# A hybrid encoder block: the norm's scale behind the input product, and the MLP's joints in another program order

## The chip, the cores and the metric

The kernel runs on one core of one Trainium2 chip. Its engines are TensorE (PE, with its weight loads as PEld), VectorE (DVE), ScalarE (ACT), GpSimd (POOL) and SyncE (SP), which here only issues transfers. The metric is the device time of one execution in microseconds.

## The reference, cut to what matters

One layer over x of 1024 rows and 1024 columns, float32. Two branches read the same product z, an attention with latent projections and a two-sided gated delta rule; their gated sum goes through `w_out` and is added to x, and a squared-ReLU MLP with its own norm follows.

```python
h = _rmsnorm(x, norm1_w[l])
z = h @ w_in[l]                      # 1024 x 4528, split into c_q, c_kv, k_r, gdn_qkv, gates ...
q_nope, q_rope = q[..., :MLA_NOPE], _rope(q[..., MLA_NOPE:], positions)
o_a = _mla_attention(q_nope, q_rope, k_nope, k_rope, v_a)
qkv = jax.nn.silu(conv(gdn_qkv))     # 5 taps along the rows
sol = lax.linalg.triangular_solve(a_mat, rhs, ...)   # inside the chunked delta rule
x = x + merged @ w_out[l]
h2 = _rmsnorm(x, norm2_w[l])
x = x + jnp.square(jax.nn.relu(h2 @ w_ff1[l])) @ w_ff2[l]
return _rmsnorm(x, final_norm_w)
```

## The kernel before

Everything is kept transposed: features on the 128 partitions, the 1024 rows of x along the free axis, so a tile is 128 x 1024. A float32 product is made from rounded parts: `split` (L169) casts an operand to its rounded half on ScalarE and takes the rest on VectorE, `wtile` (L144) does the same to a weight tile, and `mm3` (L159) sums three passes, high by high, high by low, low by high: 48 matmuls of 512 columns for a tile of z. A matmul on float32 operands that are not rounded is run as two instructions.

The 36 tiles of z come from `z_tile`. The first two are multiplied from the unrounded x while x is still arriving, and their results are scaled with `r1`, the inverse root mean square of each row (L247). For the others x is first scaled (L251) and split. What each tile is used for is a step (`s_k`, `s_v`, `s_q` convolve; `s_g` is a gate; `lora_norm` the latent parts; `s_m` the small rest); `ORDER` is the list of steps, one letter each. The v and q tiles and the latent parts are first copied out of PSUM by ScalarE (L270), the gates are activated straight from PSUM (L533); the k tiles are convolved out of PSUM (tiles 0 and 1 from their scaled copy). `s_s` and `s_i` are the triangular solve on VectorE (L519, L521); its result goes through DRAM (`d_x`) and comes back in `s_z`, whose first product is L661. `s_r` makes the rotary tables on 64 partitions of 1024 columns (L431 is its inner step) and stores them through ScalarE's queue. Pools with a fixed count of tiles (`mem` 35, `fill` 5, six half tiles) decide when a transfer may begin, and each engine works off a list that is fixed ahead.

The MLP multiplies half-size blocks with seven products instead of eight (`Visit`, with `order` naming them); `run` prepares the weights three products ahead (L1107, L1108). Sixteen visits make the hidden activations, `ff1_done` combines, squares and stores them to `d_u`. Products go in order 1, 5, 2, 3, 6, 7, 4 in the first visit. Then `plain` loads the activations of blocks 12 and 13 and eight whole products of 24 matmuls use them (L1415); fifteen visits of growing and shrinking depth follow, whose activations `u_prep` loads (L1322) and splits (L1323, L1324); the last two blocks are multiplied in four `PIECES` of 256 rows, each followed by the final norm (`finish`, L1451 to L1458).

## Time and profile before

| | |
|---|---|
| median of 3 runs | 1679.72 us (1675.71 to 1683.51) |
| the profiled execution | 1680.28 us, span 1678.6 us |
| TensorE busy | 1609.9 us |
| VectorE, ScalarE, GpSimd busy | 1206.8, 806.4, 222.8 us |
| mean granted clock of TensorE | 0.984 |

Times in rows are microseconds from the start of the span. A matmul's end is modelled, so neighbouring matmuls overlap in the rows, and the distance of their starts is what one costs. `L157` is a line of the kernel, often that of a helper; names such as `ps_z` are tiles, with their numbers left out. "[4.25 <-ACT u L1248]" is idle time of the engine before the row, and what ended it. SPq, ACTq and POOL rows of kind DMA are issues of transfers.

### The profile page before, as it was taken

Reading aid. Unit: us, or ns where it says so; the run is one execution under the profiler, and the core shown is the slowest. Engines: PE = TensorE matmul, PEld = TensorE weight load, DVE = VectorE, ACT = ScalarE, POOL = GpSimd, SP = SyncE. Lnnn points to the kernel's source line nnn. Section 1 sums busy time; section 2 is a strip of 40 time slices with the busy share of each in tenths; the row PEclk is TensorE's granted clock in tenths of the full one; section 3 lists DMA queues with packets and bytes.
Section 4 is the critical chain, followed back from the end, with each engine's and each line's share of the span. In section 5 each row is a group of like instructions: output and inputs, shape, how many; then the busy total and the mean of one; then the engine's idle time right before and its main releaser. Section 6 shows DMA issues by size and latency. Waiting matters only on the chain.

```text
span 1678.6 us, 21771 instructions
## 1 busy us (share of the span) xinstructions
PE 1609.9 (96%) x8201; PEld 1329.0 (79%) x8201; DVE 1206.8 (72%) x1751; ACT 806.4 (48%) x1365; POOL 222.8 (13%) x247
## 2 busy tenths in 40 slices
PE   8899999999989889999999998999999998999997
PEld 3687788877768877888878886888888777888886
DVE  5987999931335668888887668767776478788766
ACT  5567431441335558878762345444444443444333
POOL 1212100000003446545300000000000000000012
PEclk9999999999989999999999999999999999999998
DMA  4135243472234252111074211444343543444213
GB/s 180 62 108 132 80 163 113 139 213 88 76 101 132 57 163 89 39 39 39 26 250 138 89 50 56 164 149 152 138 165 118 190 167 113 163 163 145 82 57 101
DMA packets 85657, 196.87 MB, mean 117 GB/s; under 512 B 20128, under 2 KB 35744, under 8 KB 85296
## 3 DMA queue, kind: packets, MB, share of 16 engines
q1 hardware_dynamic: 61376, 153.95, 27.4%
q10 hardware_dynamic: 23360, 38.02, 6.5%
q0 software_dynamic: 816, 3.51, 1.0%
q8 instruction: 65, 1.06, 0.3%
q14 instruction: 40, 0.33, 0.1%
HBM read 135.22 MB, written 60.23 MB: 116 GB/s over the span
## 4 chain that ended last, share of the span: by engine, by line
PE 77%; DVE 9%; DMA 6%; ACT 4%; POOL 2%; issue 2%; ACTq 0%; SPq 0%; DVEq 0%; POOLq 0%
PE ps_z L157 15%; PE ps_af L1119 10%; PE ps_ay L1119 8%; PE ps_w L157 5%; PE ps_cf L1119 5%; PE ps_p L157 5%; PE ps_s L849 5%; PE ps_cy L1119 4%; PE ps_pv L891 4%; PE ps_pt L872 3%; PE ps_df L1119 2%; PE ps_y L157 2%; DMA f<-d_vl 2%; PE ps_y L1470 2%; PE ps_dy L1119 2%
## 5 line engine op out<-in xcount | busy, mean ns | idle before, releaser
L157 PE MATMUL ps_z<-u,wi_h 128*128 128x512 f32 x1088 | 258.0, 392 | 11.8 <-POOL u L171 2.9
L157 PEld LDWEIGHTS ps_z<-u,wi_h 128*128 128x128 f32 x1088 | 202.2, 188 | 58.7 <-ACT u L170 4.5
L1119 PE MATMUL ps_af<-u,f_w 128*128 128x512 f32 x768 | 182.4, 390 | 4.3 <-ACT u L1248 4.3
L1119 PEld LDWEIGHTS ps_af<-u,f_w 128*128 128x128 f32 x768 | 144.1, 188 | 34.9 <-ACT u L1248 5.1
L1119 PE MATMUL ps_ay<-u,y_w 128*128 128x512 f32 x576 | 140.5, 393 | 2.4 <-ACT y_w L1107 1.2
L157 PE MATMUL ps_z<-u,wi_l 128*128 128x512 f32 x544 | 136.2, 401 | 0.0
L1119 PEld LDWEIGHTS ps_ay<-u,y_w 128*128 128x128 f32 x576 | 108.3, 189 | 27.1 <-ACT y_w L1107 2.4
L1478 POOL TENSOR_TENSOR u<-u,q 128x256 f32<-128x256 f32 x20 | 15.3, 767 | 822.2 <-ACT q L1477 821.9
L157 PEld LDWEIGHTS ps_z<-u,wi_l 128*128 128x128 f32 x544 | 104.4, 194 | 22.2
L849 PE MATMUL ps_s<-u,u 128*128 128x512 f32 x384 | 104.9, 406 | 2.0 <-POOL u L838 1.4
L150 DVE TENSOR_TENSOR wi_l<-wi_r,wi_h 128x1024 fp32r<-128x1024 f32 x34 | 41.5, 1220 | 77.0 <-PE ps_z L157 61.5
L1119 PE MATMUL ps_cf<-u,f_w 128*128 128x512 f32 x384 | 95.3, 398 | 0.0
L852 DVE TENSOR_REDUCE sx<-ps_s 128x1 f32<-128x1024 f32 x64 | 77.9, 1218 | 19.5 <-PE ps_s L849 17.5
L854 ACT ACTIVATE u<-ps_s,sx 128x1024 f32<-128x1024 f32 x64 | 72.3, 1130 | 31.8 <-DVE sx L852 31.4
L1119 PEld LDWEIGHTS ps_cf<-u,f_w 128*128 128x128 f32 x384 | 73.6, 192 | 16.3 <-issue 0.5
L878 DVE TENSOR_TENSOR u<-ps_pt,u 128x512 fp32r<-128x512 f32 x128 | 82.2, 679 | 5.1 <-ACT u L877 5.1
L148 ACT CAST wi_h<-wi_r 128x1024 fp32r<-128x1024 f32 x34 | 35.7, 1050 | 104.0 <-PE ps_z L157 95.6
L856 POOL TENSOR_SCALAR u<-u,sx 128x1024 f32<-128x1024 f32 x64 | 72.4, 1135 | 84.7 <-DVE sx L855 81.9
L849 PEld LDWEIGHTS ps_s<-u,u 128*128 128x128 f32 x384 | 67.5, 189 | 14.1 <-POOL u L838 2.2
L1108 DVE TENSOR_TENSOR f_w<-f_r,f_w 128x512 fp32r<-128x512 f32 x48 | 33.1, 690 | 58.4 <-ACT f_w L1107 58.4
L1243 ACT ACTIVATE u<-u 128x512 f32<-128x512 f32 x64 | 40.5, 633 | 71.1 <-DVE u L1242 70.2
L1119 PE MATMUL ps_cy<-u,y_w 128*128 128x512 f32 x288 | 71.3, 391 | 2.5 <-DVE y_w L1108 2.1
(376 smaller groups left out, 3307.3 us busy)
## 6 DMA issues: line engine op xcount, KB each, us to landing
u<-d_u SPq DMA_DIRECT2D x36, 512.0 KB, 3.6
wi_r<-w_in SPq DMA_DIRECT2D x34, 512.0 KB, 3.5
f_r<-w_ff SPq DMA_DIRECT2D x32, 512.0 KB, 3.2
d_u<-u SPq DMA_DIRECT2D x24, 512.0 KB, 4.0
d_z<-f ACTq DMA_DIRECT2D x20, 512.0 KB, 3.2
f<-d_z SPq DMA_DIRECT2D x20, 512.0 KB, 4.2
y_r<-w_ff SPq DMA_DIRECT2D x18, 512.0 KB, 3.8
d_u<-u ACTq DMA_DIRECT2D x16, 512.0 KB, 2.6
```

The source lines that it names most:

```text
L148: A.copy(hi, raw)
L150: V.tensor_tensor(lo, raw, hi.bitcast(F32), ALU.subtract)
L157: T.matmul(ps[:, sl], w, x[:, sl], start=start, stop=stop)
L849: T.matmul(pss[:, sl], a.r[:, qsl], b.r[:, sl], start=i == 0, stop=i == 2)
L852: V.tensor_reduce(sx[:, 0:1], pss, AX.X, ALU.max, negate=True)
L854: A.activation(P.ap, pss, AF.Exp, bias=sx[:, 0:1], accum_out=sx[:, 1:2])
L856: G.tensor_scalar(P.ap, P.ap, sx[:, 1:2], 1.0, ALU.mult, ALU.mult)
L872: T.transpose(pt[:, k * 128:(k + 1) * 128], P.ap[:, ko:ko + 128], ident)
L878: V.tensor_tensor(lv, p3, hf_, ALU.subtract)
L891: T.matmul(pso[:, 0:256], VC[kb].r[:, h * 128:(h + 1) * 128], PT[kg][i].r[:, k * 256:(k + 1) * 256], start=kb == 0 and i == 0, stop=kb == ...
L1119: T.matmul(ps, w[:, a, k * 128:(k + 1) * 128], self.xops[k][i].parts[b], start=n == 0 and i in FIRST, stop=n == 3 * self.g - 1, skip_group ...
L1243: A.activation(t, t, AF.Square)
```

## The change

Two edits at once. The first: x is only multiplied with the norm's weight and split as it arrives, and all tiles of z are made from that with three rounded passes; `r1` is applied to each result when it leaves PSUM (`z_scaled`, on VectorE). Tiles 0, 1 and 2 are multiplied from the start, in one loop, the third in banks of the smaller pool; the sums for `r1` come behind tile 1. The weight tile 1 is loaded behind x3, and its cast stands behind that of x4. The k tiles are convolved from SBUF; their squares are taken from PSUM. With it the rotary angles are made on 128 partitions of 256 columns and their tables stored by ten transfers from GpSimd's queue, the root of the score scale going to either side.

The second: in the MLP's first visit the last squares of the norm come ahead of the fourth product and the norm ahead of the fifth, with the steps that need its result held back; the activations for the plain products are loaded in the last visit of the first half and split beside its products; of the eight plain products two are put into the first two visits behind; the last piece has its own ending, with the columns' weights applied ahead, the norm's sum in two parts, four outputs of double width and two queues. All loads of `d_u` are issued by GpSimd instead of SyncE.

The core of the first edit:

```diff
+    xt, xs = [], []
+    w0 = wraw(w_in[0], "wi0")
     for k in range(8):
...
         xt.append(mem.alloc())
         nc.sync.dma_start(xt[k].ap, xT[k * 128:(k + 1) * 128, :])
...
-    pz = [pa("ps_z0"), pa("ps_z1")]
-    for i, k in [(i, k) for k in range(K0) for i in range(2)] + \
-            [(i, k) for i in range(2) for k in range(K0, 8)]:
-        mm_pass(pz[i], w0[i][:, k * 128:(k + 1) * 128], xt[k].ap, k == 0, k == 7)
-    psn = [pb("ps_n1a"), pb("ps_n1b")]
+        if k == 3:
+            w1 = wraw(w_in[1], "wi1")
...
+    casts = []
+    early = [wsplit(w0, "wi0")]
+    for k in range(8):
+        h, l = mem.pair()
+        for sl in (HS if k < 2 else [slice(0, 1024)]):
+            cast = A.activation(h.r[:, sl], xt[k].ap[:, sl], AF.Copy, scale=pcol(N1 + k))
+            V.scalar_tensor_tensor(l.r[:, sl], xt[k].ap[:, sl], pcol(N1 + k), h.ap[:, sl],
+                                   ALU.mult, ALU.subtract)
+        xs.append((h, l))
+        casts.append(cast)
+        if k == 4:
+            early.append(wsplit(w1, "wi1"))
     acc = fill.alloc()
     for k in range(8):
         sq = acc if k == 0 else fill.alloc()
         last = A.activation(sq.ap, xt[k].ap, AF.Square)
+        tc.add_manual_dep(last.ins, casts[7].ins.name, nosync, reason="order")
+        xt[k].free()
...
-    with tc.high_priority(1000):
-        for i, t in enumerate((acc, sq)):
-            for sl, ps in zip(HS, psn):
-                T.matmul(ps, ones, t.ap[:, sl], start=i == 0, stop=i == 1)
...
-    zb = big("ZB")
-    zb = [zb[:, 0:1024], zb[:, 1024:2048]]
-    for ps, z in zip(pz, zb):
-        V.tensor_tensor(z, ps, r1.ap, ALU.mult)
...
-        xn = fill.alloc()
-        V.scalar_tensor_tensor(xn.ap, xt[k].ap, pcol(N1 + k), r1.ap, ALU.mult, ALU.mult)
-        h, l = mem.pair()
-        split(h, l, xn.ap, G if k % 2 else V)
-        xn.free()
...
+    r1 = mem.alloc()
+    pz = []
+    for i in range(3):
+        ps = [pa(f"ps_z{i}")] if i < 2 else [pb(f"ps_z{i}a"), pb(f"ps_z{i}b")]
+        pz.append([ps[0][:, 0:HALF], ps[0][:, HALF:2 * HALF]] if i < 2 else ps)
+    early.append(wtile(w_in[2], "wi2"))
...
+    def z_pass(i, k, p, q):
+        for s, sl in enumerate(HS):
+            T.matmul(pz[i][s], early[i][p][:, k * 128:(k + 1) * 128], xs[k][q].r[:, sl],
+                     start=p + q + k == 0, stop=p == 1 and k == 7)
+
+    for i in range(3):
+        if i == 0:
+            for k in range(8):
+                for j in range(2):
+                    z_pass(j, k, 0, 0)
+                    z_pass(j, k, 0, 1)
+        for k in range(8):
+            if i == 2:
+                z_pass(i, k, 0, 0)
+                z_pass(i, k, 0, 1)
+        for k in range(8):
+            z_pass(i, k, 1, 0)
+        if i == 1:
+            psn = [pb("ps_n1a"), pb("ps_n1b")]
+            for j, t in enumerate((acc, sq)):
+                for sl, ps in zip(HS, psn):
+                    T.matmul(ps, ones, t.ap[:, sl], start=j == 0, stop=j == 1)
+            acc.free()
+            sq.free()
+            for j in range(2):
+                rsqrt(r1.ap[:, HS[j]], psn[j], 1.0 / D, eps_t[:, 0:1], half("m"), half("t"),
+                      None if j else last)
...
     def z_tile(i):
-        if i < 2:
...
+
+        if i < 3:
+            return zip(HS, pz[i])
+        with tc.high_priority(200):
+            w = wtile(w_in[i], f"wi{i}")
         ps = pa(f"ps_z{i}")
         mm3(ps, w, 0, xs)
-        return ps
...
+        return [(slice(0, 1024), ps)]
+
+    def z_scaled(dst, i):
+        for sl, ps in z_tile(i):
+            with tc.high_priority(200):
+                V.tensor_tensor(dst[:, sl], ps, r1.ap[:, sl], ALU.mult)
+
+    def conv_tile(dst, i, ch):
+
+        zt = fill.alloc()
+        z = zt.ap
+        z_scaled(z, i)
...
-        if slow:
-            zt.free()
+        zt.free()
...
             A.copy(t.ap[:, HS[q]], pst)
+            if sums is not None:
+                junk = half("j")
+                for n in range(4):
+                    cs, c = slice(n * C, (n + 1) * C), h * N + q * 4 + n
+                    kn_last[:] = [A.activation(junk[:, cs], pst[:, cs], AF.Square,
+                                               accum_out=sums[:, c:c + 1])]
         A.dma_start(dram[h], t.ap)
...
     def s_k(h):
         conv_tile(kT[h].ap, h, 4 + h)
-        t = stack(kT[h], h, d_ks)
-        for n in range(N):
-            ins = A.activation(t.ap[:, n * C:(n + 1) * C], t.ap[:, n * C:(n + 1) * C], AF.Square,
-                               accum_out=kn[:, h * N + n:h * N + n + 1])
...
+        t = mem.alloc()
+        pin, an, tq, neg = (t.ap[:, i * 256:(i + 1) * 256] for i in range(4))
+        nc.sync.dma_start(pin.bitcast(I32), pos)
+        V.tensor_copy(an, pin.bitcast(I32))
+        V.tensor_scalar(an, an, pcol(FREQ), None, ALU.mult)
...
-        A.dma_start(d_rt[0], rte.ap)
-        A.dma_start(d_rt[1, 0:64], rte.ap[64:128])
-        A.dma_start(d_rt[1, 64:128], rte.ap[0:64])
-        rte.free()
-        tn.free()
+        V.tensor_scalar(an, an, math.sqrt(SCALE), None, ALU.mult)
+        V.tensor_scalar(neg, an, -1.0, None, ALU.mult)
+        c = mem.alloc()
+        G.memset(c.ap[0:64, :], math.sqrt(SCALE))
+        for i in range(2):
+            o = 64 - 64 * i
+            G.dma_start(d_rt[i, 64 - o:128 - o], c.ap[0:64])
+            for j, src in enumerate((an[0:64], an[0:64], neg[q64], an[q64])):
+                G.dma_start(d_rt[i, o + j * 16:o + j * 16 + 16].rearrange("f (q t) -> (f q) t", q=4), src)
...
+        ang.append(mem.alloc())
+        nc.sync.dma_start(ang[0].ap[q64], d_rt[0, q64])
...
     def s_g(i):
-        ps = z_tile(16 + i)
         t = fill.alloc()
-        late[0] = A.activation(t.ap, ps, AF.Silu if i < 4 else AF.Sigmoid)
+        z_scaled(t.ap, 16 + i)
+        late[0] = A.activation(t.ap, t.ap, AF.Silu if i < 4 else AF.Sigmoid)
```

`z_tile`'s users `s_m`, `s_v`, `s_q`, `lora_norm` change as `s_g` does. The core of the second:

```diff
+        if m < 7:
+            add_square(m)
...
-    for _ in x_odd(3):
-        pass
+    xo = x_odd(3)
+    next(xo)
...
+    def plain_load(j0):
+
+        ul = []
+        for f in range(4):
+            a, b = mem.pair()
+            for q, sl in zip(((0, 3), (0, 2))[f % 2], HS):
+                G.dma_start(b.ap[:, sl], d_u[j0 + f // 2, q, :, RT if q or f % 2 else LT])
+            ul.append((a, b))
+        return ul
...
+    scaled, waiting = [], []
+
+    def act(t, src, half_):
+        if not scaled:
+            waiting.append((t, src, half_))
+            return
+        V.scalar_tensor_tensor(t, src, 0.0, r2.ap[:, half_], ALU.max, ALU.mult)
+        A.activation(t, t, AF.Square)
...
     def each1(v, i):
-        if v.name == "f0" and i == v.order[1] and not state1[0]:
-            state1[0] = True
+        if v is f0 and i == v.order[3]:
+            for _ in xo:
+                pass
+            add_square(7)
+        if v is f0 and i == v.order[4]:
             norm2()
+            scaled.append(True)
+            for w in waiting:
+                act(*w)
...
+        if v is vs[-1]:
+            q = v.order.index(i)
+            if q:
+                for xt_ in XT:
+                    xt_[v.order[q - 1]].free()
+            if q == 2:
+                ul0.extend(plain_load(NP2))
+                splits0.append(plain_split(ul0))
+            if q > 2:
+                next(splits0[0])
...
-                nc.sync.dma_start(lo.ap, d_u[j, q])
+                G.dma_start(lo.ap, d_u[j, q])
...
-                nc.sync.dma_start(t.ap[:, RT], d_u[j, q, :, LT])
+                G.dma_start(t.ap[:, RT], d_u[j, q, :, LT])
...
+        if q in (0, 1) and i == v.order[1]:
+            next(pp)
+        if not preps and nextj[0] < NP2 and nextj[0] - len(freed) < LIVE and mem.live + 7 <= NUNIT:
             preps.append(u_prep(nextj[0]))
...
-    ul = plain(NP2)
-    for mp in range(4):
-        w = wtile(w_ff2t[0, mp], f"w2_{mp}")
-        for m in (2 * mp, 2 * mp + 1):
-            ps = pa(f"ps_y{m}")
-            mm3(ps, w, m % 2 * 4, ul)
-            V.tensor_tensor(Y[m], ps, Y[m], ALU.add)
-            for _ in range(2):
-                if not preps and nextj[0] < 3:
...
+    def plain_products():
+        ul = ul0
+        for mp in range(4):
+            if mp < 3:
+                w = wtile(w_ff2t[0, mp], f"w2_{mp}")
+            for m in (2 * mp, 2 * mp + 1):
+                ps = pa(f"ps_y{m}")
+                mm3(ps, w if mp < 3 else [x.r for x in w3], m % 2 * 4, ul)
+                V.tensor_tensor(Y[m], ps, Y[m], ALU.add)
+                if m == 7:
+                    for t in w3 + [x for p in ul for x in p]:
+                        t.free()
+                yield
+
+    pp = plain_products()
+    for m in range(6):
+        next(pp)
+        for _ in range(2):
...
+    raw = wp.tile([128, 1024], F32, tag="wraw", name="w2_3r", bufs=3)
+    nc.sync.dma_start(raw, w_ff2t[0, 3])
+    w3 = list(mem.pair())
+    split(*w3, raw)
...
+
+
+    t0, t1 = PIECES[-1]
+    sl, n = slice(t0, t1), t1 - t0
+    yn = [x.rearrange("p (m c) -> p m c", m=2) for x in
+          (t.ap[:, q * 512:(q + 1) * 512] for t in (mem.alloc(), mem.alloc()) for q in range(2))]
+    for m in range(8):
+        piece(sl, n, m)
...
+        A.activation(yn[m // 2][:, m % 2], Y[m][:, sl], AF.Copy, scale=pcol(NF + m))
...
+    psn = pb("ps_n4")[:, 0:n]
+    T.matmul(psn, ones, xsq.ap[:, sl], start=True, stop=False)
+    T.matmul(psn, ones, sq, start=False, stop=True)
+    r, a_, b_ = r3.ap[:, sl], half("m")[:, 0:n], half("t")[:, 0:n]
+    V.tensor_scalar(a_, psn, 1.0 / D, eps_t[:, 0:1], ALU.mult, ALU.add)
+    A.activation(r, psn, AF.Ln, bias=eps_t[:, 0:1], scale=1.0 / D)
+    A.activation(r, r, AF.Exp, scale=-0.5)
+    A.activation(b_, r, AF.Square)
+    V.scalar_tensor_tensor(b_, b_, -0.5, a_, ALU.mult, ALU.mult)
+    V.scalar_tensor_tensor(r, b_, 1.5, r, ALU.add, ALU.mult)
+    ov = out.rearrange("(m p) s -> p m s", p=128)
+    for q in range(4):
+        V.tensor_tensor(yn[q], yn[q], bcm(r, 2), ALU.mult)
+        (A if q % 2 else nc.sync).dma_start(ov[:, 2 * q:2 * q + 2, sl], yn[q])
```

`plain_split` splits one pair at each call; `piece` is the loop body of the pieces' product, unchanged.

## Rows read from the trace of the kernel before

**Rows 1.** Busy us (count) by stretch: length, engines, granted clock, DMA share, GB/s.

```profile
41.00:62.00 21.00, 15.52 (x61) 11.08 (x62) 21.00 (x14) 7.83 (x9) 10.14 (x3) 1.00 0.08 26
190.00:350.00 160.00, 157.61 (x698) 129.33 (x697) 155.90 (x174) 61.83 (x64) 1.03 (x2) 1.00 0.41 138
485.00:500.00 15.00, 10.51 (x47) 7.71 (x46) 5.89 (x5) 3.65 (x4) 0.00 (x0) 0.89 0.75 211
1016.00:1036.00 20.00, 15.74 (x54) 11.35 (x53) 18.54 (x29) 15.07 (x27) 0.00 (x0) 0.83 0.08 26
1327.00:1344.00 17.00, 12.82 (x46) 9.21 (x46) 8.99 (x11) 8.02 (x9) 0.00 (x0) 0.90 0.98 340
1380.00:1398.40 18.40, 13.55 (x47) 8.80 (x45) 16.99 (x29) 8.78 (x18) 0.00 (x0) 0.91 0.39 129
1415.00:1615.00 200.00, 200.00 (x884) 165.47 (x883) 155.69 (x239) 76.46 (x115) 0.00 (x0) 1.00 0.39 128
```

**Rows 2.** The chain that ended last: start, us, what.

```profile
294.94 54.40 PE ps_z L157 x240
...
486.27 11.65 DMA f<-d_x
```

**Rows 3.** Timeline of TensorE: start, us, instruction, count [idle before].

```profile
6.35 15.86 PE L157 MATMUL ps_z<-u,wi_r 128*128 128x512 f32 x30 [6.35 <-DMA u<-xT]
...
25.48 14.76 PE L157 MATMUL ps_z<-u,wi_r 128*128 128x512 f32 x34
...
61.59 4.92 PE L157 MATMUL ps_z<-u,wi_h 128*128 128x512 f32 x21
```

**Rows 4.** Timeline of ScalarE and VectorE at the start.

```profile
6.23 1.06 ACT L230 ACTIVATE f<-u 128x1024 f32<-128x1024 f32 x1 [2.79 <-DMA u<-xT]
...
18.59 1.06 ACT L230 ACTIVATE f<-u 128x1024 f32<-128x1024 f32 x1 [0.22 <-DMA u<-xT]
...
30.36 0.69 DVE L192 SCALAR_TENSOR_TENSOR f<-t,f 128x512 f32<-128x512 f32 x1
...
40.13 1.21 DVE L247 TENSOR_TENSOR ZB<-ps_z,f 128x1024 f32<-128x1024 f32 x1
```

**Rows 5.** Groups of instructions: count | busy us, mean ns | idle before.

```profile
L431 DVE SCALAR_TENSOR_TENSOR u<-u,u 64x1024 f32<-64x1024 f32 x8 | 9.8, 1222 | 0.3
...
L461 POOL DMA_DIRECT2D d_g<-u x8 | 5.7, 714 | 31.1 <-ACT u L458 30.2 <-issue 1.0
```

**Rows 6.** Timeline of VectorE and TensorE around the solve's end and first use.

```profile
344.73 0.22 DVE L521 TENSOR_TENSOR SY<-SY,f 128x62 f32<-128x62 f32 x1
...
407.41 0.24 PE L661 MATMUL ptz<-ident,f 64*64 64x64 f32 x1
```

**Rows 7.** Timeline of TensorE at the joints of the MLP.

```profile
1030.47 0.79 PE L1119 MATMUL ps_af<-u,f_w 128*128 128x512 f32 x1 [4.25 <-ACT u L1248]
...
1333.13 4.47 PE L157 MATMUL ps_y<-u,w_h 128*128 128x512 f32 x12 [3.19 <-ACT u L170]
```

**Rows 8.** Timeline of VectorE, TensorE and SyncE in the last piece.

```profile
1666.17 0.41 DVE L1472 TENSOR_TENSOR f<-ps_y,f 128x256 f32<-128x256 f32 x1
...
1667.60 1.22 PE L1451 MATMUL ps_n<-u,ones 128*128 128x256 f32 x2 [2.59 <-DVE u L1478]
...
1671.61 1.67 DVE L1456 SCALAR_TENSOR_TENSOR YB<-YB,par,u 128x256 f32<-128x256 f32 x4
...
1674.02 1.87 SPq L1458 DMA_DIRECT2D outT<-f  x4
```

**Rows 9.** DMA issues: queue, count, KB each, median us to landing.

```profile
u<-d_u SPq DMA_DIRECT2D x36, 512.0 KB, 3.6
...
SY<-d_g POOLq DMA_DIRECT2D x2, 1024.0 KB, 10.1
d_x<-SY SPq DMA_DIRECT2D x4, 512.0 KB, 7.2
...
d_g<-u POOLq DMA_DIRECT2D x8, 128.0 KB, 2.8
```

More of the change, by code (lines that the diff above doesn't have):

```diff
@@ L233, in block_kernel @@
             sq.free()
-    with tc.high_priority(1000):
-        for i, t in enumerate((acc, sq)):
-            for sl, ps in zip(HS, psn):
-                T.matmul(ps, ones, t.ap[:, sl], start=i == 0, stop=i == 1)
-    acc.free()
-    sq.free()
-    r1 = fill.alloc()
-    for i in range(2):
-        rsqrt(r1.ap[:, HS[i]], psn[i], 1.0 / D, eps_t[:, 0:1], half("m"), half("t"),
-              None if i else last)
-    zb = big("ZB")
-    zb = [zb[:, 0:1024], zb[:, 1024:2048]]
-    for ps, z in zip(pz, zb):
-        V.tensor_tensor(z, ps, r1.ap, ALU.mult)
@@ L500, in s_v @@
         vT[h] = mem.alloc()
-        conv_tile(vT[h].ap, 5 + h, 8 + h, slow=True)
+        conv_tile(vT[h].ap, 5 + h, 8 + h)
     def s_S(h):
-        stack(vT[h], h, d_vs).free()
+        stack(vT[h], h, d_vs)
         vT[h].free()
@@ L702, in block_kernel @@
         l.free()
+    r1.free()
     KST, VST = [mem.alloc() for _ in range(H)], [mem.alloc() for _ in range(H)]
@@ L1171, in ff1_raw, with add_square @@
         return [w_ff1[j, q].rearrange("p (a c) -> p a c", a=2) for q in range(2)]
+    def add_square(m):
+        for sl in HS:
+            if m == 0:
+                A.activation(xsq.ap[:, sl], Y[m][:, sl], AF.Square)
+            else:
+                sq = half("q")
+                A.activation(sq, Y[m][:, sl], AF.Square)
+                V.tensor_tensor(xsq.ap[:, sl], xsq.ap[:, sl], sq, ALU.add)
     f0 = Visit("f0", EARLY, ff1_raw(0), XT, None)
@@ L1301, in block_kernel @@
     for xt_ in XT:
-        for t in xt_[1:]:
-            t.free()
+        xt_[vs[-1].order[-1]].free()
     r2.free()
@@ L1436, in block_kernel @@
                 t.free()
-    ul = plain(NP2 + 2)
+    ul = plain_load(NP2 + 2)
+    for _ in plain_split(ul):
+        pass
     w2 = []
@@ L1458, in finish, with piece @@
             nc.sync.dma_start(out[m * 128:(m + 1) * 128, sl], Y[m][:, sl])
+    def piece(sl, n, m):
+        wh, wl = w2[m // 2]
+        ps = pb(f"ps_y{m}_{sl.start}")
+        for j, (w, i) in enumerate(((wh, 0), (wh, 1), (wl, 0))):
+            for k in range(4):
+                o = ((m % 2) * 4 + k) * 128
+                T.matmul(ps[:, 0:n], w[:, o:o + 128], ul[k][i].r[:, sl], start=j + k == 0,
+                         stop=j == 2 and k == 3)
+        V.tensor_tensor(Y[m][:, sl], ps[:, 0:n], Y[m][:, sl], ALU.add)
     rest = iter(())
-    for t0, t1 in PIECES:
+    for t0, t1 in PIECES[:-1]:
         sl, n = slice(t0, t1), t1 - t0
         for m in range(8):
-            wh, wl = w2[m // 2]
-            ps = pb(f"ps_y{m}_{t0}")
-            for j, (w, i) in enumerate(((wh, 0), (wh, 1), (wl, 0))):
-                for k in range(4):
-                    o = ((m % 2) * 4 + k) * 128
-                    x = ul[k][i].r
-                    T.matmul(ps[:, 0:n], w[:, o:o + 128], x[:, sl], start=j + k == 0,
-                             stop=j == 2 and k == 3)
-            V.tensor_tensor(Y[m][:, sl], ps[:, 0:n], Y[m][:, sl], ALU.add)
+            piece(sl, n, m)
             if m == 0:
```

126 lines of the change are left out of this document (45 added, 81 removed).

## Prediction

> **What bounds it now.** I read the busy time by stretch first, then the chain that ended last, and at last the engine timelines around the places where TensorE stands still. In the long stretches TensorE never stops: 200.00 of 200 us between 1415 and 1615 [rows 1]. So this kernel gets faster in two ways only: less work on TensorE, or shorter holes in it. The chain gives the price of full work: 240 matmuls of 512 columns on rounded operands in 54.40 us, 0.2267 us each [rows 2]. With that price a stretch tells its own hole: its length less its count times 0.2267. The stretches that matter are the start and four joints of the MLP [rows 1]. The granted clock is 1.00 where TensorE runs on and 0.83 to 0.91 in the three holes inside the MLP: after some us of idling it falls from 2.4 towards 1.2 GHz, so that a hole also makes the matmuls behind it slow. The holes below hold both parts.
>
> **The start.** Before, TensorE multiplies tiles 0 and 1 with unrounded operands: 64 instructions, 34 of them in 14.76 us, 0.434 each [rows 3]. That is 64 x 0.434 = 27.8 us for 32 products of 512 columns, two passes each. Then it waits for x to be scaled by the norm and split again: between 41 and 62 us it holds 61 matmuls, 13.8 us of work in 21 [rows 1]. At 61.59 the tile after the next is running [rows 3]; by counting, tiles 0 to 2, the norm's sums and 11 matmuls of tile 4 are done.
>
> After, these are 3 x 48 + 11 = 155 matmuls at 0.2267 = 35.1 us, and the norm's 8 instructions at 0.434 = 3.5: 38.6 us. Against what was there (27.8 + 3.5 + 59 x 0.2267 = 44.7) that is 6.1 us less work, because three rounded passes are cheaper than two slow double ones. When can it begin? x0 was in SBUF at 6.23 us and x7 at 18.59, the later ones 1.28 us apart [rows 4]. The whole of weight tile 0 now comes ahead of x0 (384 KB more, about 1 us), and a cast of half a tile some 0.6 us (a step over a whole one takes 1.06 [rows 4]): first matmul near 8.3. Weight tile 1 comes behind x3, so x4 lands where it did, near 14.7; the cast of tile 1 stands behind that of x4: 14.7 + 1.06 + 1.04 = 16.8. Until then tile 0 can use x0 to x4, 30 matmuls, 6.8 us, if the order lets it run ahead; as the loop is written, TensorE waits after 4 of them (0.9 us). From 16.8 on nothing is late, for x7 is split by about 21.9. So the same point is reached at 16.8 + 38.6 - 6.8 = 48.6 or at 54.5, instead of 61.59: a gain of 13.0 or 7.1. I take **10**, the middle, since the order on TensorE is a list that is fixed ahead, and was seen to put work forward (the chain's pieces change places), but not by how much.
>
> The norm's result is no longer on this path: it is first wanted when tile 0 leaves PSUM. It was ready at 31.05 [rows 4] and will be at 41 to 47 (the sums now wait for tiles 0 and 1), while tile 4 wants the first bank near 46. That costs nothing to 2 us, and is inside the spread above.
>
> What is paid: each z tile leaves PSUM through VectorE with the scale on it, 1.21 us for 1024 columns [rows 4], 34 more than before: 41 us. Taken away are 8 scalings of x (1.2 us alone, up to 3.4 beside GpSimd) and three quarters of the rotary angles (a step of 1.22 us on 1024 columns of 64 partitions [rows 5] becomes one of 256 on 128, by the ratio of columns about 0.4: some 20 such steps, 14 us saved). ScalarE loses 12 copies. The cover for the 41 us is that VectorE's long job, the triangular solve, is early: its last step was at 344.73, and the first product that needs it at 407.41 [rows 6], 63 us later. The store to DRAM between them lands in 7.2 us [rows 9]; with the load back I count 12. Even with all 41 us ahead of it, it would eat the 50 that are left only when TensorE arrives 10 us earlier. I cost it at 0; without that cover it is up to the 10 gained. A tile waits in PSUM at most until the tile after the next begins, 10.9 us (48 x 0.2267), and VectorE's steps are about 1.2 us long, so the scale need not stop TensorE. The rotary tables' stores go from ScalarE's queue to GpSimd's, 10 issues of 0.71 us each [rows 5], ahead of the small stores of the solve; the tables' rows are wanted 60 us later: 0.
>
> **The joints of the MLP.** By the count in each stretch [rows 1]:
>
> At 1016 to 1036 us 54 instructions hold 50 matmuls (11.3 us) and four norm passes (1.7): hole 7.0. Named is a 4.25 us wait for a copy on ScalarE out of the first bank [rows 7], which stood behind the norm's chain of eight ScalarE steps and two squares. The change puts the squares behind three products and the norm behind four, so that chain gets 10.9 us of cover. ScalarE was 75% busy there and VectorE 93%, so not all of it closes: **5.5** of 7.0 (ends 3 and 7).
>
> At 1327 to 1344: 46 matmuls, 10.4 us, hole 6.6, a wait for the cast of the loaded activations, whose loads were issued behind the last store [rows 7]. They are loaded now while the last visit runs, from rows stored two visits before, and split under its products. The cast stands in ScalarE's order ahead of weight casts; a late load would hold those. **5** (ends 3 and 6.6).
>
> At 1380 to 1398.4: 47 matmuls, 10.7 us, hole 7.7. Small products of 3 to 6 matmuls wait for their weights, and VectorE is 92% busy. Two products of 24 matmuls (5.44 us each) now stand inside this stretch. They add no work to VectorE there beyond their own two sums; but it must also prepare the activations that the earlier eight products covered. **5** (ends 2 and 7.7).
>
> The last piece: the last sum on VectorE ends at 1666.58, the norm's product begins at 1667.60 and takes 1.22, the outputs' scaling begins at 1671.61 in eight steps, and their eight issues run on SyncE to 1675.89 [rows 8]; the span ends 2.7 later. After, the first part of the norm's product doesn't wait for the last square, one sum on VectorE goes (0.43), one ScalarE step runs beside the others (0.4), and four steps of 512 columns and four issues on two queues take the place of eight and eight: 1.0 + 0.4 + 1.6 = **3** (ends 1.5 and 3.5).
>
> The loads of d_u move from SyncE's queue to GpSimd's, which is idle there. SyncE's land 3.6 us after issue at 512 KB; GpSimd's took 2.8 at 128 KB and 10.1 at 1 MB in rows that are not contiguous [rows 9]. These bound it; I take about 5, the middle by size. It hides, since loads are issued some activations ahead: 0.
>
> The Trainium skill's "DMA: Bandwidth & Descriptors" (Anatomy of one DMA) gives for this queue a fixed 2.0 us and the bytes at 436 GB/s: an estimate of 3.2 us for 512 KB, where the rows leave 2.8 to 10.1. No row here shows that size on that queue. By the page the loads would be no later than SyncE's and rival (d) below would hold next to nothing; by the rows it keeps its chance, and the sum is the same by both.
>
> **Sum.** 10 + 5.5 + 5 + 5 + 3 = 28.5 us off the profiled execution's 1680.28 (span 1678.6 and 1.7 around it; the median of the runs, 1679.72, is 0.6 lower): **1651.8, say 1652**. With all the low ends 16.6 (1664), with all the high ones 37.8 (1642).
>
> **Rivals.** (a) VectorE takes the start's gain back: scales wait behind the solve's steps, or the solve ends so late that its products wait. For it: between 190 and 350 us it is 97% busy (155.90 of 160) [rows 1]. Against: the 50 us above. It decides when the solve ends over 40 us later. Time: 1652 + 10 = 1662.
> (b) The joints don't close, because VectorE and ScalarE, not the order, are their limit. For it: 93% and 92% in two of them. Then only the low ends come: 3 + 3 + 2 + 1.5 + 10 = 19.5, 1661.
> (c) Better: the hole at 485 to 500, a load of 11.65 us [rows 2] that collides with loads of 2 MB while the clock falls to 0.89, goes too when buffers come free earlier. 47 instructions, many of them short, so at most 7 us: 1645; with high ends elsewhere 1636.
> (d) Slower: the loads on GpSimd's queue come late. ScalarE is busy 76 us of 200 in 1415 to 1615 [rows 1], 7.3 of each visit's 19.0 us (84 x 0.2267), so 11.7 are free for four loads' waits, 2.9 each; were nothing issued ahead, a landing above 3.6 + 2.9 = 6.5 us would stop TensorE. At 10.1 us that is 4 x 3.6 = 14 us in each of ten visits, 140 us; at 7.5, 40 us: 1692. Against: loads are issued ahead, and the 1 MB row is twice the size.
> (e) No change: the fixed order of one edit pushes another's work back, gains and losses within 8 us: 1676.
>
> **How the numbers follow.** The forecast's case, 1642 to 1664, holds 0.57; (a) and (b) 0.12 and 0.12; (c) 0.07; (d) 0.06; (e) 0.06. A measurement of this kernel tells about 0.5% from nothing, 8.4 us: faster means under 1671. Faster: 0.57 + 0.12 + 0.12 + 0.07 less a little for (a) and (b) together, 0.87; same 0.07; slower 0.06. The range leaves out (d), (e) and the ends of the others: 1637 to 1670.
>
> **What would show it.** Right: rounded matmuls from about 8 us on and tile 4 running near 50; the first product of the solve's result about 10 us earlier; no hole over 2 us at the MLP's joints and a clock of 1.00 there; the end 10.5 us after the last main product. Wrong: TensorE waiting for VectorE's scale steps between 60 and 350 us, ScalarE's casts waiting for d_u loads longer than before with weight casts behind them, or the scan's beginning not moved by the gain at the start.

## The result and the profile after

The changed kernel takes **1654.75 us** (median of 4 runs, 1652.12 to 1656.64) where the kernel before took 1677.72 in the same comparison: ratio 0.9864, interval 0.9844 to 0.9885, 23 us less. The forecast was 1652, range 1637 to 1670. The profiled execution has a span of 1653.8 us, 24.8 under that of before. The page's first part after:

```profile
span 1653.8 us, 21952 instructions
PE 1601.6 (97%) x8235; PEld 1335.7 (81%) x8235; DVE 1213.9 (73%) x1781; ACT 790.7 (48%) x1360; POOL 257.0 (16%) x317
```

**Where the 24.8 us came from.** The same product is looked up in both traces, and the difference of its starts is what has been won up to there. TensorE's timeline before, at the first product of the latent keys and at the MLP's first product:

```profile
349.18 1.07 PE L157 MATMUL ps_kk<-u,wkv_h 128*128 128x512 f32 x4
...
1015.85 2.88 PE L1119 MATMUL ps_af<-u,f_w 128*128 128x512 f32 x12
```

and the chain that ended last before, at the end of the second visit, in the second half and at the last piece:

```profile
1060.65 5.44 PE ps_af L1119 x24
...
1419.84 2.72 PE ps_dy L1119 x12
...
1645.89 11.50 PE ps_y L1470 x96
```

TensorE's timeline after, with the start:

```profile
8.38 6.86 PE L258 MATMUL ps_z<-u,wi_h 128*128 128x512 f32 x16 [8.38 <-ACT u L233]
...
16.69 10.74 PE L258 MATMUL ps_z<-u,wi_h 128*128 128x512 f32 x46 [0.21 <-ACT wi_h L221]
...
48.87 5.60 PE L156 MATMUL ps_z<-u,wi_h 128*128 128x512 f32 x24
...
344.30 1.07 PE L156 MATMUL ps_kk<-u,wkv_h 128*128 128x512 f32 x4
...
401.07 0.24 PE L692 MATMUL ptz<-ident,f 64*64 64x64 f32 x1
...
1006.47 2.88 PE L1151 MATMUL ps_af<-u,f_w 128*128 128x512 f32 x12
```

and the chain after, at the same three products:

```profile
1043.89 5.44 PE ps_af L1151 x24
...
1394.62 2.72 PE ps_dy L1151 x12
...
1621.97 11.50 PE ps_y L1540 x96
```

| reached | before | after | won so far |
|---|---|---|---|
| 11 matmuls of tile 4 done | 61.59 [rows 3] | 48.87 + 11 x 0.2267 = 51.4 | 10.2 |
| latent keys | 349.18 | 344.30 | 4.9 |
| first product of the solve's result | 407.41 [rows 6] | 401.07 | 6.3 |
| MLP's first product | 1015.85 | 1006.47 | 9.4 |
| end of the second visit | 1060.65 | 1043.89 | 16.8 |
| second half, past the small visits | 1419.84 | 1394.62 | 25.2 |
| last piece | 1645.89 | 1621.97 | 23.9 |
| end of the span | 1678.6 | 1653.8 | 24.8 |

The start gives 10.2 and half of it is gone by 344 us. The first joint adds 7.4, the second and third 8.4. Then 1.3 is lost, and the last piece adds 0.9.

**The joints by stretches**, columns as in [rows 1]. A stretch of before (1310, 1350, 1531) is laid on one of after by the 16.76 us won up to there. Before:

```profile
1310.00:1350.00 40.00, 35.82 (x148) 28.21 (x148) 20.52 (x25) 19.31 (x26) 0.00 (x0) 0.96 0.54 190
1350.00:1425.00 75.00, 70.13 (x296) 55.60 (x295) 61.70 (x96) 27.05 (x45) 0.00 (x0) 0.98 0.42 146
1531.00:1591.00 60.00, 60.00 (x266) 49.70 (x265) 45.64 (x69) 22.82 (x33) 0.00 (x0) 1.00 0.34 110
```

After, with the first joint ahead of them:

```profile
1005.00:1025.00 20.00, 20.00 (x86) 15.73 (x85) 18.86 (x30) 15.80 (x28) 0.00 (x0) 1.00 0.16 52
1293.24:1333.24 40.00, 37.17 (x157) 30.30 (x157) 24.18 (x28) 19.98 (x27) 9.98 (x19) 0.96 0.80 294
1333.24:1408.24 75.00, 74.01 (x324) 60.25 (x323) 63.81 (x100) 28.39 (x47) 4.80 (x9) 1.00 0.33 109
1514.24:1574.24 60.00, 58.78 (x259) 48.14 (x258) 42.92 (x66) 20.29 (x31) 5.90 (x11) 1.00 0.30 99
```

The hole is the length less the count times 0.2267. At the first joint TensorE is busy all 20 us at a clock of 1.00, where it was 15.74 at 0.83 [rows 1]. The second joint's hole goes from 6.4 only to 4.4, the third's from 7.9 to 1.5, and a stretch that had none (266 x 0.2267 = 60.3) now has 1.3.

**What waits at the second joint and near 1550.** Timeline after:

```profile
1316.11 0.38 SPq L1122 DMA_DIRECT2D y_r<-w_ff  x1
...
1325.39 0.29 DVE L1128 TENSOR_TENSOR s<-y_r 128x128 f32<-128x128 f32 x1 [7.62 <-DMA y_r<-w_ff]
1325.61 1.22 DVE L1478 TENSOR_TENSOR YB<-ps_y,YB 128x1024 f32<-128x1024 f32 x1
...
1326.88 5.51 PE L156 MATMUL ps_y<-u,w_h 128*128 128x512 f32 x16 [2.83 <-DVE YB L1478]
...
1543.05 0.56 DVE L1129 TENSOR_TENSOR s<-y_r,s 128x384 f32<-128x384 f32 x1 [2.52 <-DMA y_r<-w_ff]
...
1551.10 2.98 PE L1151 MATMUL ps_ay<-u,y_w 128*128 128x512 f32 x12 [1.22 <-DVE YB L1418]
```

A weight load of a small visit is issued at 1316.11 and used at 1325.39. VectorE stands at the step that needs it, 0.29 us of work, for 7.62 us. The plain product's sum is queued behind that step, and TensorE waits for the bank that the sum frees. Near 1550 it is the same in small. This wait took the place of the one that was removed.

**What waits near 183 us.** Timeline after, GpSimd, VectorE and TensorE:

```profile
162.50 16.80 POOL L512 TENSOR_SCALAR_AFFINE_SELECT SY<-SY 128x1024 f32<-128x1024 f32 x4 [20.76 <-DVE SY L511]
...
179.34 0.27 DVE L551 TENSOR_TENSOR f<-SY 128x62 f32<-128x62 f32 x1 [4.34 <-POOL SY L512]
...
182.09 1.22 DVE L297 TENSOR_TENSOR f<-ps_z,u 128x1024 f32<-128x1024 f32 x1
...
183.46 9.12 PE L156 MATMUL ps_z<-u,wi_h 128*128 128x512 f32 x32 [2.79 <-DVE f L297]
```

The solve's first step waits on VectorE 4.34 us for GpSimd. The scale of a gate tile stands behind it (L297 at 182.09), and TensorE waits 2.79 us for that tile's bank. The 32 matmuls behind take until 192.41, 8.95 instead of 32 x 0.2267 = 7.25, so another 1.7 goes to the clock: the granted clock from 183.46 to 192.41 is 0.81.

**The last piece.** Timeline after, VectorE, TensorE and ScalarE's queue:

```profile
1642.81 0.41 DVE L1542 TENSOR_TENSOR f<-ps_y,f 128x256 f32<-128x256 f32 x1
...
1643.79 0.79 PE L1580 MATMUL ps_n<-q,ones 128*128 128x256 f32 x2
...
1647.45 2.50 DVE L1590 TENSOR_TENSOR u<-u,u 128x512 f32<-128x512 f32 x4
...
1648.78 1.60 ACTq L1591 DMA_DIRECT2D outT<-u  x2
```

From the last sum's end (1643.22) to the last issue's end (1650.38) are 7.2 us; before it was 1666.58 to 1675.89, 9.3 [rows 8]. But from the last issue to the end it is now 3.4 instead of 2.7, and the last sum itself comes 0.6 later behind the last main product. From the end of the last main product to the end of the span are 12.7 us, where before it was 13.6.

### The profile page after: what moved, and what is told of

Its sections match the earlier page's. It is cut to its first block, busy times and chain, and to the rows that moved or that the text cites. A ratio compares the mean times of both kernels' runs of the same rounds, so it can differ in the third digit from the quotient of the medians.

```text
span 1653.8 us, 21952 instructions
## 1 busy us (share of the span) xinstructions
PE 1601.6 (97%) x8235; PEld 1335.7 (81%) x8235; DVE 1213.9 (73%) x1781; ACT 790.7 (48%) x1360; POOL 257.0 (16%) x317
## 4 chain that ended last, share of the span: by engine, by line
PE 73%; DVE 9%; DMA 4%; ACT 3%; POOL 2%; issue 2%; ACTq 0%; DVEq 0%; SPq 0%; POOLq 0%
PE ps_z L156 10%; PE ps_af L1151 10%; PE ps_ay L1151 7%; PE ps_w L156 5%; PE ps_p L156 5%; PE ps_cf L1151 5%; PE ps_s L881 5%; PE ps_pv L923 4%; PE ps_cy L1151 4%; PE ps_pt L904 3%; PE ps_df L1151 3%; PE ps_y L1540 2%; PE ps_y L156 2%; PE ps_dy L1151 2%; DMA f<-d_vl 2%
## 5 line engine op out<-in xcount | busy, mean ns | idle before, releaser
L156 PE MATMUL ps_z<-u,wi_h 128*128 128x512 f32 x1056 | 254.6, 397 | 6.4 <-DVE f L297 3.3
L156 PEld LDWEIGHTS ps_z<-u,wi_h 128*128 128x128 f32 x1056 | 199.4, 190 | 51.4 <-issue 5.2
L156 PE MATMUL ps_z<-u,wi_l 128*128 128x512 f32 x528 | 129.8, 396 | 0.0
L156 PEld LDWEIGHTS ps_z<-u,wi_l 128*128 128x128 f32 x528 | 99.7, 190 | 21.1
L1275 POOL DMA_DIRECT2D u<-d_u x16 | 8.7, 547 | 484.4 <-DMA w_r<-w_ff2t 472.2
L297 DVE TENSOR_TENSOR f<-ps_z,u 128x1024 f32<-128x1024 f32 (+1 forms) x36 | 41.7, 1160 | 48.4 <-PE ps_z L156 48.3
L309 DVE SCALAR_TENSOR_TENSOR u<-f,par,u 128x1022 f32<-128x1022 f32 (+1 forms) x48 | 64.6, 1363 | 12.7 <-ACT u L305 12.0
```

Source lines behind the costliest of these rows:

```text
L156: T.matmul(ps[:, sl], w, x[:, sl], start=start, stop=stop)
L297: V.tensor_tensor(dst[:, sl], ps, r1.ap[:, sl], ALU.mult)
L309: V.scalar_tensor_tensor(dst[:, d0:d1], z[:, d0 + o:d1 + o], pcol(c + t), dst[:, d0:d1], ALU.mult, ALU.add)
```

## The experiments

Executions of the same instructions differ. In nine profiles with the first edit and nothing else changed ahead of the MLP, its first product comes at 1002.7 to 1009.2 us, mean 1006.0; in the two without it at 1015.85 and 1012.53. So a span is not read to better than some 3 us, and I read each place by its own rows. Spreads of times stand in the intervals, all against the kernel before. The changed kernel's is 0.9844 to 0.9885; only four versions lie clear of it (each edit alone, the norm early again, and the solve's first step moved behind), and what is said of the others rests on rows.

**Each edit alone.**

The first edit's lines in the kernel before, with the MLP untouched:

```diff
+        for k in range(8):
+            z_pass(i, k, 1, 0)
...
+                V.tensor_tensor(dst[:, sl], ps, r1.ap[:, sl], ALU.mult)
...
```

and the second edit's lines in the kernel before, with all ahead of the MLP untouched:

```diff
+            add_square(7)
...
+                ul0.extend(plain_load(NP2))
...
+            next(pp)
...
```

> Only the first edit (input product on split rows, scale behind it, rotary tables), the MLP as before. If the two edits act in places of their own, the MLP begins where it does with both, at 1006.6 us of the span instead of 1015.9, and everything behind runs as before: span 1678.6 - 9.4 = 1669.2. Rival: the early gain only holds together with the other edit; then the MLP begins at 1010 or later and the span is 1673 or more.

> Only the second edit (norm later, loads ahead, two products interleaved, last piece, loads of d_u from GpSimd). If the edits add up, the span is 1678.6 - (24.8 - 9.4) = 1663.2, of which 7.4 come at the MLP's first visit. Rival: part of it needs the first edit; then it lies above 1666.

The first edit alone: 1670.17 us, ratio 0.9961 (0.9946 to 0.9976). The MLP begins at 1005.31, and at the first joint TensorE waits as before:

```profile
1019.92 0.79 PE L1151 MATMUL ps_af<-u,f_w 128*128 128x512 f32 x1 [4.25 <-ACT u L1280]
```

The second alone: 1661.77, ratio 0.9915 (0.9897 to 0.9934). The product of the two ratios is 0.9876, and both together gave 0.9864: within the intervals the edits add up. By the times the first edit alone is worth 6.5 us (4.0 to 9.1), by the means of the MLP's beginning 1014.2 - 1006.0 = 8.2; the 9.4 of the table is one pair of executions.

**The norm early again.**

```diff
-        if m < 7:
-            add_square(m)
+        add_square(m)
...
-        if v is f0 and i == v.order[4]:
+        if v is f0 and i == v.order[1]:
             norm2()
```

> The changed kernel with the squares and the norm back ahead of the second product. By the theory that this chain held ScalarE's copy out of the first bank, TensorE waits about 4 us in the first visit again and the hole of 7.4 us is back: span 1661.2. Rival: the hole was closed by what else moved there, and little comes back: 1654 to 1657.

1663.48 us, ratio 0.9917 (0.9892 to 0.9943). TensorE waits again, and the end of the second visit is reached 1.0 us ahead of before, counted from the MLP's first product, instead of 7.4: 6.4 of 7.4 come back.

```profile
1018.48 0.79 PE L1151 MATMUL ps_af<-u,f_w 128*128 128x512 f32 x1 [4.21 <-ACT u L1303]
```

**All eight plain products first.**

```diff
-    for m in range(6):
+    for m in range(8):
         next(pp)
...
-        if q in (0, 1) and i == v.order[1]:
-            next(pp)
```

> The changed kernel with all eight plain products ahead of the fifteen visits. By the theory that the two products of 24 matmuls cover the small visits, the waits between 1362 and 1394 come back, 6.8 us: span 1660.6. Rival: that hole closed because the activations are loaded earlier; then the span stays within 2 us of 1653.8.

1657.48 us, ratio 0.9883 (0.9869 to 0.9898), and at the third joint:

```profile
1335.94:1410.94 75.00, 71.93 (x311) 57.41 (x310) 62.27 (x98) 28.30 (x47) 3.78 (x8) 1.00 0.32 99
```

The hole is 75 - 311 x 0.2267 = 4.5, not 7.9 and not 1.5. So the two products are worth 3.0 of the 6.4 us; the other 3.4 stay without them. What else moved there is the earlier loading and splitting of the plain activations and the queue of the d_u loads; which of them holds the 3.4 was not told apart, but with the loads back on SyncE's queue (next) this hole is 2.9, so about 1.4 of it may go with the queue. Both theories were half right. This is one profile, but the hole at this joint is 1.5 in all eight profiles that have the two products between the visits and all these loads on GpSimd's queue. The hole at the second joint was 2.6 in this run.

**The d_u loads back on SyncE.**

```diff
-                G.dma_start(lo.ap, d_u[j, q])
+                nc.sync.dma_start(lo.ap, d_u[j, q])
...
```

> The changed kernel with all loads of d_u issued by SyncE again. If the queue costs nothing, as the prediction had it, the joint at 1310 to 1350 and the stretch near 1550 keep their holes (4.4 or 2.6, and 1.3 us) and the span stays within 2 us of 1653.8. Rival 1: on GpSimd's queue the loads compete with the weight loads on SyncE's, so that the weights of the small visits come late; then both holes shrink by 1 to 3 us. Rival 2: behind the waiting loads on SyncE the weights come later still, and the holes grow by 2 us or more.

1652.20 us, ratio 0.9840 (0.9819 to 0.9861). The stretches that answer to those of after:

```profile
1289.49:1329.49 40.00, 40.00 (x178) 33.10 (x178) 27.34 (x33) 20.07 (x28) 0.00 (x0) 1.00 0.63 208
1329.49:1404.49 75.00, 73.40 (x318) 59.06 (x317) 63.99 (x100) 30.88 (x50) 0.00 (x0) 1.00 0.48 159
1510.49:1570.49 60.00, 60.00 (x267) 49.67 (x266) 42.94 (x71) 19.47 (x32) 0.00 (x0) 1.00 0.29 96
```

Holes 0, 2.9 and 0 instead of 4.4, 1.5 and 1.3: rival 1, and the third hole grew by 1.4, which no theory named. The queue was not free. With the loads on GpSimd's queue, beside the weight loads on SyncE's, the second joint's stretch has a DMA share of 0.80 and 294 GB/s; with all of them in SyncE's list it has 0.63 and 208. The step on the late weights then waits 0.95 us instead of 7.62. In this kernel the first sum also came out ahead of that step on VectorE, so queue and order both changed there; the next run takes the order by itself. Near 1550 the hole is 0.8 to 1.7 in the nine profiles with these loads on GpSimd's queue and gone in the three with them on SyncE's (this run and both versions with several mends below). The times alone don't separate this run from the changed kernel: the intervals overlap.

**The plain sums ahead of the step on the weights.**

```diff
+    vs[0].after = lambda ins: tc.add_manual_dep(ins.ins, adds[2].ins.name, nosync, reason="order")
...
             ins = V.tensor_tensor(s3, a11, a21, ALU.subtract)
+            if self.after:
+                self.after(ins)
```

> The changed kernel, in which VectorE takes the first step on the loaded weights of the first visit behind three of the plain sums instead of ahead of the first. By the theory that this step waits for a late load with the sums queued behind it, TensorE's wait of 2.8 us at the second joint goes and the hole there falls from 4.4 (2.6 in other executions) below 1.5. Rival: the transfers are saturated there and the splits of the activations are late too; then another wait takes its place and the hole stays above 2.

1651.57 us, ratio 0.9841 (0.9824 to 0.9859):

```profile
1295.27:1335.27 40.00, 40.00 (x178) 33.11 (x178) 27.32 (x33) 20.07 (x28) 9.97 (x19) 1.00 0.80 294
1335.27:1410.27 75.00, 74.03 (x324) 60.23 (x323) 65.16 (x101) 30.54 (x50) 5.35 (x10) 1.00 0.36 120
1516.27:1576.27 60.00, 58.38 (x257) 47.75 (x256) 41.50 (x67) 19.22 (x30) 5.37 (x10) 1.00 0.29 93
```

One step on VectorE, of 0.29 us, stands in another place; the order of all other instructions is the same on every engine. The DMA share is 0.80 and 294 GB/s as in the changed kernel, and the hole at the second joint is gone (178 matmuls in 40 us). So the transfers, however full, did not stop TensorE there; the order on VectorE did. The third joint stays at 1.5, and near 1550 a hole of 1.7 stays: there it is the queue and not this step.

**One gate tile scaled ahead of the solve.**

```diff
-ORDER = "kkkmrvGGklGtvSvvGsciiSigiigcSSg..."
+ORDER = "kkkmrvGGklGtvSvvGscSgiiiiigcSSg..."
...
+            if j == 1:
+                tc.add_manual_dep(ins.ins, scaled_g[0].ins.name, nosync, reason="order")
```

> The changed kernel, in which the first gate tile is scaled ahead of the solve's first step on VectorE, which waits for GpSimd. By the theory that this queue costs the early gain, TensorE's wait at 183 us falls from 2.8 to under 1, the clock behind it stays at 1.00, and the norm of the latent tile comes at 195 to 197 instead of 199 to 201. The MLP then begins 1 to 4 us earlier if that carries through, and no earlier if the loads of the solve's result take it back.

1656.09 us, ratio 0.9867 (0.9841 to 0.9892). The wait at 183 us is gone, and a longer one stands at the latent tile's norm:

```profile
197.63 2.93 PE L589 MATMUL ps_ck<-q,ones 128*128 128x512 f32 x3 [4.51 <-ACT q L588]
```

The latent keys come at 344.54. The wait moved, which the expectation had not named: the scale of the last latent tile ran at 195.70, among the solve's steps that now stood ahead of it. The MLP began at 1003.68, within the spread of the nine. The solve's first step did not wait for GpSimd in this run; the last section shows what GpSimd did.

**The gates without the scale.**

```diff
-        z_scaled(t.ap, 16 + i)
-        late[0] = A.activation(t.ap, t.ap, AF.Silu if i < 4 else AF.Sigmoid)
+        for sl, ps in z_tile(16 + i):
+            late[0] = A.activation(t.ap[:, sl], ps, AF.Silu if i < 4 else AF.Sigmoid)
```

> The changed kernel, in which the twenty gate tiles leave PSUM through ScalarE alone, without the norm's scale (left out of the computation): 24 us less on VectorE between 180 and 500 us. By the theory that the scale steps cost half of the early gain, TensorE's waits between 183 and 230 us go and the first product of the latent keys comes at 341 or earlier instead of 344 to 346. By the same theory the loads of the solve's result have already hidden that loss, so the MLP begins no earlier than with the scale, 1002 to 1009. Rival: what is won carries through, and it begins before 1002.

1651.87 us, ratio 0.9851 (0.9830 to 0.9872), and the latent keys at 345.80, no earlier. TensorE waits longer at the same place, now for ScalarE:

```profile
187.65 9.17 PE L156 MATMUL ps_z<-u,wi_h 128*128 128x512 f32 x32 [3.82 <-ACT f L565]
```

So my theory of this moment, that the cost of the scale steps takes half of the early gain, falls. The load on VectorE is not it: 24 us less changed nothing up to 346. The solve's first step waited 4.33 us for GpSimd again. What stood behind the solve's first step here were the latent tiles' steps, behind them ScalarE's casts, and behind those the gate's activation. The MLP began at 1001.45, by the letter the rival's case, but only 1.3 below the lowest of the nine. What is won lies behind the solve: from its first product to the attention's first score 195.6 us pass, against 198.6 to 203.4 in the nine.

**The solve's first step behind all of them.**

```diff
-ORDER = "kkkmrvGGklGtvSvvGsciiSigiigcSSg..."
+ORDER = "kkkmrvGGklGtvSvvGscSggciiiiiSSg..."
...
+            if z0 == 11:
+                scaled_c.append(ins)
...
+            if j == 1:
+                tc.add_manual_dep(ins.ins, scaled_c[0].ins.name, nosync, reason="order")
```

> The changed kernel, in which the solve's first step stands on VectorE behind the scales of two gate tiles and of the last latent tile (it waits there for GpSimd until 179 us). By the theory that this one waiting step holds what stands behind it, TensorE's waits of 2.8 us at 183 and 1.2 at 199 both go and the first product of the latent keys comes at 342 or earlier instead of 344 to 346. Rival: VectorE and ScalarE are full there, and a wait of the same size comes behind another step, as when only the first gate was put ahead; then it comes at 344 to 346 again. Whether the MLP then begins before 1002 shows if it carries through.

**1644.51 us, ratio 0.9801 (0.9784 to 0.9819)**, below the interval of the changed kernel: the fastest version here. Both waits are gone, and TensorE's timeline reads:

```profile
338.85 1.07 PE L156 MATMUL ps_kk<-u,wkv_h 128*128 128x512 f32 x4
...
996.36 2.88 PE L1156 MATMUL ps_af<-u,f_w 128*128 128x512 f32 x12
```

The latent keys are 10.3 us ahead of before, the whole gain of the start, and the MLP begins 9.6 us ahead of the mean of 1006.0. It carries through. The solve itself ends later, 363.0 against 358.3, and that costs nothing: its first product comes at 394.79. The edit moves more than one step: five pieces of the solve stand behind the scales, and with them the order of other steps on VectorE and ScalarE changed, while TensorE's is the same. So the place of the solve's beginning is shown as the cause, and not the one waiting step by itself.

**The last piece.**

```diff
-        if m > 1:
+        if m:
             next(rest, None)
```

> The changed kernel, in which the outputs of the third piece are scaled one product earlier, so that none of them stands ahead of the last sum on VectorE. If that queue costs 0.6 us, the last sum ends 1.6 us behind the last main product instead of 2.1, and the span from there to the end is 12.1 instead of 12.7. Rival: the sum waits for TensorE, and 12.7 stays.

1654.32 us, ratio 0.9855 (0.9837 to 0.9872). The last sum now ends at 1642.21. The last main product is modelled to end at 1640.48, so the sum is 1.7 behind it instead of 2.1, and the end 12.3 instead of 12.7: 0.4 of the 0.6 us. The two versions below, which have the same mend, end 12.3 behind it too; the nine profiles with the changed kernel's last piece end 12.6 to 13.3 behind it.

**Two versions of the later mends together**, both without the mend at the solve: the order of the sums, the earlier scaling, and the d_u loads on GpSimd's queue for the first activations only (blocks 12 and 13 for the plain products, 0 to 3 for the visits); and all of them on SyncE's with the earlier scaling.

```diff
-                G.dma_start(lo.ap, d_u[j, q])
+                (G if j < 4 else nc.sync).dma_start(lo.ap, d_u[j, q])
...
```

> The changed kernel with what the runs point to: VectorE's first step on the loaded weights behind three plain sums, the loads of d_u on GpSimd's queue only for the first four activations and on SyncE's for the rest, the third piece's outputs scaled one product earlier. If the holes at the second joint (4.4 or 2.6), near 1550 (1.3) and in the last piece (0.4) go, it ends 4 to 6 us before the changed kernel: ratio to the kernel before 0.982 to 0.984. Rival: the joint behind grows by what is won; then 0.986.

> The changed kernel with all loads of d_u issued by SyncE and the third piece's outputs scaled one product earlier. The holes are 0, 2.9 and 0 at the second joint, the third and near 1550 as they were with SyncE's loads alone, against 4.4, 1.5 and 1.3: some 4 us before the changed kernel, ratio to the kernel before 0.983 to 0.985. Rival: the difference was one execution's; then 0.986.

1649.79 us, ratio 0.9839 (0.9817 to 0.9861), and 1651.49, ratio 0.9839 (0.9818 to 0.9860). The first one's stretches:

```profile
1291.53:1331.53 40.00, 40.00 (x178) 33.11 (x178) 27.31 (x33) 20.07 (x28) 9.93 (x19) 1.00 0.80 293
1331.53:1406.53 75.00, 73.06 (x320) 59.42 (x319) 64.57 (x101) 30.62 (x50) 1.07 (x2) 1.00 0.36 119
1512.53:1572.53 60.00, 60.00 (x266) 49.68 (x265) 42.94 (x70) 19.86 (x31) 0.00 (x0) 1.00 0.29 93
```

The holes at the second joint and near 1550 are gone, and the third grew from 1.5 to 2.5. By these rows that is 4.4 + 1.3 - 1.0 = 4.7 us. In the second version the holes are 0, 3.1 and 0, nearly as with SyncE's loads alone. Both ratios lie where they were expected, but the intervals of the times still overlap that of the changed kernel. These mends together with the one at the solve were not run.

## Why the prediction was right, and where it was not

The total, 1652 against 1654.75, is right, and most of the gain came from the start and the joints, as forecast. Not every term is right, and that the total came within 3 us is partly luck. Two of the signs that the prediction named show it: TensorE did wait for a scale step between 60 and 350 us (at 183), and the first product of the solve's result came 6.3 us earlier instead of about 10.

- **The start**: 10 forecast, 10.2 measured. The first matmul came at 8.38 (8.3 forecast), tile 0 ran 18 matmuls ahead of tile 1's weights (the two ends were 4 and 30), and from 16.69 on nothing was late.
- **The scale at nothing**: the step that failed. The text took the solve's 50 us of slack and the 1.2 us length of the steps for the cover. Length and load were not the price: in the order on VectorE the scale stands behind a step that waits for GpSimd. That step waits because GpSimd's selects took 16.8 us where they had taken 7.7: from 162.50 and 170.33, when their inputs were ready, they would at the old length have ended near 174 (an estimate: 170.33 + 3.61), and VectorE came to the step at 175.0. Rival (a) named this place ("scales wait behind the solve's steps"), but tied it to an end of the solve over 40 us later; that end came 13.4 later, 358.3 against 344.9, and 5 of the 10 us were still gone at 344. Moving the solve's beginning gave 5.5 back there. By the means of the nine profiles that run is ahead by 6.4 at the latent keys (345.3), 7.3 at the solve's first product (402.1), 9.5 at the attention's first score (603.1 against 593.6) and 9.6 by the MLP; the 2 between solve and attention lie within what that stretch varies by itself.
- **What hid it**: by the MLP 9.4 was left, since a wait near 359 shrank from 1.58 to 0.39 and the hole behind f<-d_x in 485 to 500 shrank from 4.5 us of waiting to 1.1. That is rival (c) in part. Two errors, about 5 us each, cancelled; the forecast held neither, so that is luck.
- **First joint**: 5.5 forecast, 7.4 measured. The whole hole closed; the fear that ScalarE and VectorE would keep part of it was not borne out.
- **Second joint**: 5 forecast, 2.0 measured. The hole that is left has two sizes in the profiles with the loads on GpSimd's queue and the sums where they were: 4.2 to 4.4 at a clock of 0.96 in this one and three others, and 1.7 to 2.8 at 1.00 in four, which makes 3.6 to 4.7 won. The sign named for this joint, no hole over 2 us, failed in seven of the eight. The wait that took the place of the removed one was a weight load, not looked at in the forecast: it feared a late load ahead of ScalarE's casts, and it stood on VectorE.
- **Third joint**: 5 forecast, 6.4 measured, 3.0 of it by the two products.
- **The d_u loads on GpSimd's queue**: costed at 0. They landed in 4.0 us at 512 KB (about 5 forecast, 3.5 from SyncE), and rival (d) did not come; the list of DMA issues after:

```profile
u<-d_u POOLq DMA_DIRECT2D x36, 512.0 KB, 4.0
...
y_r<-w_ff SPq DMA_DIRECT2D x18, 512.0 KB, 4.6
```

But beside the weight loads they made those late (4.6, against 4.1 with the d_u loads back in the same queue and 3.8 before): by the holes with SyncE, 4.4 + 1.5 + 1.3 - 2.9 = 4.3 us in this execution, the order on VectorE that went with it included; 1.6 to 2.7 by the executions whose second hole was 1.7 to 2.8. The Trainium skill's "DMA: Bandwidth & Descriptors" (Anatomy of one DMA) gave an estimate of 3.2 for one such load; the trace says 4.0, the median of 36 loads, many of which share the DMA engines with others.
- **Last piece**: 3 forecast, 0.9 measured. The chain from the last sum to the last issue shortened by 2.1 and the end followed 12.7 us after the last main product, not 10.5. The prediction left out that the span ends 3.4 behind the last issue, now of twice the width and on ScalarE's queue, instead of 2.7 (width and queue were not told apart), and that the last sum stands behind the third piece's outputs (0.6).

What the rotary tables' new shape is worth by itself was not run.

The sum 9.4 + 7.4 + 8.4 - 1.3 + 0.9 = 24.8 stands against the forecast's 28.5; the -1.3 is the new hole near 1550.

## What to carry to other kernels

When work is moved onto an engine with a fixed order, its price is not its length but what it stands behind: look for the steps ahead of it that wait for another engine, and put the waiting step last if it has slack. Where a hole is closed by loading earlier, ask which other load is then late, and on which engine the step that needs it stands ahead of work that TensorE wants. A total that comes out right can hold errors of opposite sign; comparing the start of the same product in both traces at several places shows them.
